# Casting and turning the first rows of a projection kernel between its first products

**Chip, cores, metric.** One core of a Trainium2 chip. The time is device time in microseconds (us). "Span" is the time from the first to the last instruction, about 1.8 us less.

## The reference

```python
batch, seq, hidden = 16, 512, 768
x     = randn(batch, seq, hidden)      # float32, 8192 rows
w_qkv = randn(hidden, 3 * hidden)      # float32
qkv = np.matmul(x, w_qkv)
out = np.stack([q, k, v])              # the three column blocks of qkv, float32
```

## The kernel before

Rows are handled in pairs of 128-row tiles. Pairs 0 to 2 are multiplied directly in bf16; pairs 3 to 31 take a path with seven block products instead of eight. Only the head, the first 20 us of some 361, is touched by the change. In it, each of the six 128-row tiles ("row 1" to "row 6") is loaded, cast to bf16, turned by TensorE (PE) with six transposes into PSUM (the memory that PE writes to), and copied out by VectorE (first three k) and ScalarE (last three). Weights for the first 512 columns come in six k-tiles of 128 x 512. Before the first rows are there, PE runs "dummies", 512-column matmuls on zeros whose results nobody reads. The program order given here is the order on each engine.

```python
def copy_halves(dst, src, two):
    nc.vector.tensor_copy(out=dst[0], in_=src[0])
    if two:
        nc.scalar.activation(dst[1], src[1], ident)
    else:
        nc.vector.tensor_copy(out=dst[1], in_=src[1])

def turn_rows(p, two=True):
    c = xc.pop(p)
    xb[p] = xb_pool.tile([P, KT, 2 * P], bf16, name="xb", tag="xb")
    for r in range(2):
        cols = c[:, r, :].rearrange("m (p j) -> m j p", j=KT)
        ps = ps_pool.tile([P, KT, P], bf16, name="ps")
        for j in range(KT):
            nc.tensor.transpose(ps[:, j, :], cols[:, j, :], eye)
        ks = (slice(0, KH), slice(KH, KT))
        copy_halves([xb[p][:, n, r * P:(r + 1) * P] for n in ks], [ps[:, n, :] for n in ks], two)

# ... loads are issued in the order rows of pair 0, pair 1, k-tiles 0 to 5, remainder weights, pair 2, ...
singles = [((0, ), (0, 1)), ((1, ), (0, 1)), ((0, 1), (2, 3))]      # (k-tiles, row tiles)
singles += [((j, ), range(4)) for j in range(2, KT)]
# ...
busy(11)                 # 11 dummy matmuls on a zero tile
cast_rows(0)
turn_rows(0)
busy(4)
cast_rows(1)
cast_k(0)
cast_k(1)
turn_rows(1)
for j in range(2, KT):
    cast_k(j)
act.activation(w_rem[1][:], st_rem[:, KH:], ident)
dve.tensor_copy(out=w_rem[0][:], in_=st_rem[:, :KH])
# ...
block(0, 0, b1[0], singles, nothing)
rem(0)                   # 12 products with the 256 remaining columns
rem(1)
cast_rows(2, False)
turn_rows(2, False)
block(0, 0, b1[0], halves((4, 5)), nothing)
# ... the next block starts here ("next block" below); pairs 3 to 31 follow after two more
```

## Time and profile before

| | before |
|---|---|
| three timed runs | 362.50, 362.59, 362.67 us |
| the profiled execution | 363.13 us, span 361.3 |
| PE busy | 353.4 us (98%) |
| VectorE / ScalarE / GpSimd busy | 62% / 51% / 48% |

The page's line of the granted TensorE clock shows 9 (90% or more) in all 40 slices. The other lines that carry the argument stand in the prediction.

### The profile page before, as it was taken

How to read it: one execution, taken by the hardware profiler on the slowest of the kernel's cores; microseconds unless marked ns; L12 is line 12 of the kernel's file. 1: busy time of each engine (PE TensorE's matmuls, PEld its weight loads, DVE VectorE, ACT ScalarE, POOL GpSimd, SP SyncE). 2: the span in 40 equal slices, each digit the busy share in tenths (PEclk: the TensorE clock that was granted, in tenths of full speed). 3: DMA queues.
4: the chain of work that ended last, by engine and by line, in shares of the span. 5: the costliest groups of instructions: out<-in, count | busy, mean ns of one | idle time of the engine just before them, and what ended most of it. 6: DMA issues, size and time to landing. Idle time of an engine off the chain costs nothing.

```text
span 361.3 us, 5221 instructions
## 1 busy us (share of the span) xinstructions
PE 353.4 (98%) x1765; PEld 251.0 (69%) x1797; DVE 224.4 (62%) x239; ACT 182.9 (51%) x304; POOL 173.9 (48%) x180
## 2 busy tenths in 40 slices
PE   8999999999999999999999999999999999999995
PEld 3644577777777777777777777777777777777763
DVE  3499826765566765566675565676556676556642
ACT  4547555455454545454545445455545454545452
POOL 0001861746664445664445665444665444666410
PEclk9999999999999999999999999999999999999999
DMA  7999869988898999899899999998989899999666
GB/s 298 405 388 373 286 221 359 331 289 295 278 328 301 294 273 294 276 324 315 280 280 290 281 308 309 291 289 278 292 288 321 295 300 271 297 272 339 264 261 232
DMA packets 80617, 108.08 MB, mean 299 GB/s; under 512 B 4816, under 2 KB 60368, under 8 KB 80592
## 3 DMA queue, kind: packets, MB, share of 16 engines
q1 hardware_dynamic: 65184, 96.35, 80.8%
q10 hardware_dynamic: 15408, 11.41, 9.6%
q8 instruction: 14, 0.23, 0.3%
q14 instruction: 11, 0.09, 0.1%
HBM read 32.24 MB, written 75.50 MB: 298 GB/s over the span
## 4 chain that ended last, share of the span: by engine, by line
PE 96%; ACT 1%; issue 1%; ACTq 0%; DVE 0%
PE ps L212 75%; PE ps L262 11%; PE ps L385 9%; PE ps L365 1%; PE ps L167 1%; ACT o L243 0%; ACTq L303 0%; ACT xb L147 0%; ACT orem L317 0%; DVE xb L145 0%; ACT xc L147 0%; ACTq L319 0%; DVE zero L346 0%; ACTq L317 0%
## 5 line engine op out<-in xcount | busy, mean ns | idle before, releaser
L212 PE MATMUL ps<-t,s 128*128 128x512 f32 x696 | 173.8, 398 | 0.0
L212 PEld LDWEIGHTS ps<-t,s 128*128 128x128 f32 x696 | 130.7, 188 | 29.7
L175 POOL CAST xb<-xf 128x1536 bf16<-128x1536 f32 x29 | 43.8, 1510 | 168.3 <-DVE xf L130 156.0
L240 DVE TENSOR_TENSOR o<-o,ps 128x512 f32<-128x512 f32 x58 | 39.9, 688 | 91.2 <-ACT o L239 91.2
L130 DVE STREAM_TRANSPOSE xf<-xin 128x1536 f32<-128x1536 f32 x29 | 85.5, 2950 | 3.7 <-DMA out_dram<-orem 2.1
L212 PE MATMUL ps<-b,xb 128*128 128x512 bf16 x320 | 82.4, 380 | 1.5
L239 ACT ACTIVATE o<-ps 128x512 f32<-128x512 f32 x58 | 34.8, 600 | 44.2 <-PE ps L212 44.2
L212 PEld LDWEIGHTS <-xb 128*128 128x128 bf16 x348 | 31.7, 98 | 35.6 <-issue 7.3
L233 ACT ACTIVATE o<-ps 128x512 f32<-128x512 f32 x58 | 34.9, 601 | 42.1 <-PE ps L212 39.4
L246 DVE TENSOR_TENSOR o<-o,ps 128x512 f32<-128x512 f32 x58 | 39.9, 688 | 21.3 <-PE ps L212 20.2
L212 PE MATMUL ps<-b,s 128*128 128x512 f32 x174 | 48.7, 389 | 0.0
L262 PE MATMUL ps<-w_rem,xb 128*128 128x256 bf16 x384 | 47.2, 273 | 0.0
L243 ACT ACTIVATE o<-ps 128x512 f32<-128x512 f32 x58 | 34.7, 599 | 24.1 <-PE ps L212 21.3
L226 ACT ACTIVATE o<-ps 128x512 f32<-128x512 f32 x58 | 34.7, 598 | 23.8 <-DVE o L246 20.6
L262 PEld LDWEIGHTS <-xb 128*128 128x128 bf16 x384 | 37.4, 98 | 11.2 <-issue 0.5
L230 DVE TENSOR_TENSOR o<-o,ps 128x512 f32<-128x512 f32 x58 | 36.5, 673 | 5.4 <-PE ps L212 4.1
L212 PEld LDWEIGHTS ps<-b,s 128*128 128x128 f32 x174 | 32.7, 188 | 6.8
L184 POOL TENSOR_TENSOR s<-s,xf 128x384 fp32r<-128x384 f32 x29 | 30.0, 1035 | 2.3
L183 POOL TENSOR_TENSOR s<-xf 128x384 fp32r<-128x384 f32 x29 | 30.9, 1064 | 0.0
L185 POOL TENSOR_TENSOR s<-xf 128x384 fp32r<-128x384 f32 x29 | 29.5, 1017 | 0.0
L187 POOL TENSOR_TENSOR s<-xf,s 128x384 fp32r<-128x384 f32 x29 | 29.5, 1016 | 0.0
L272 ACT ACTIVATE orem<-ps 128x512 f32<-128x512 f32 x31 | 18.5, 598 | 20.7 <-PE ps L262 19.5
(36 smaller groups left out, 129.4 us busy)
## 6 DMA issues: line engine op xcount, KB each, us to landing
out_dram<-o SPq DMA_DIRECT2D x62, 768.0 KB, 4.8
out_dram<-o SPq DMA_DIRECT2D x65, 256.0 KB, 4.1
xin<-in_x_dram SPq DMA_DIRECT2D x62, 192.0 KB, 6.9
xin<-in_x_dram ACTq DMA_DIRECT2D x54, 192.0 KB, 4.4
out_dram<-orem SPq DMA_DIRECT2D x31, 256.0 KB, 5.7
st<-in_w_qkv_dram SPq DMA_DIRECT2D x6, 768.0 KB, 13.1
xin<-in_x_dram SPq DMA_DIRECT2D x3, 768.0 KB, 5.7
st<-in_w_qkv_dram SPq DMA_DIRECT2D x6, 256.0 KB, 6.1
```

Of the source, the lines that this page charges most:

```text
L130: nc.vector.transpose(t[:].rearrange("p j (g b) -> p g j b", b=G), xin.pop(p)[:].rearrange("p g (a j) -> p g j a", a=G),)
L175: nc.gpsimd.tensor_copy(out=xb[p][:], in_=xf[p][:])
L212: nc.tensor.matmul(ps[:], lhs[j], rhs[j], start=(start and j == 0), stop=(j == KH - 1), skip_group_check=True,)
L226: nc.scalar.activation(c11, u.x[:], ident)
L230: nc.vector.tensor_tensor(c11, c11, u.z[:], op=add)
L233: nc.scalar.activation(c12, u.x[:], ident)
L239: nc.scalar.activation(c22, u.x[:], ident)
L240: nc.vector.tensor_tensor(c22, c22, u.y[:], op=add)
L243: nc.scalar.activation(c21, u.x[:], ident)
L246: nc.vector.tensor_tensor(c12, c12, u.y[:], op=add)
L262: nc.tensor.matmul(ps, xb[p][:, j, r * P:(r + 1) * P], w_rem[j // KH][:, j % KH, :], start=(j == 0), stop=(j == KT - 1), skip_group_check= ...
L385: nc.tensor.matmul(ps[n][:], xb[p][:, j, r * P:(r + 1) * P], w[:, j, :], start=(j == 0), stop=(j == KT - 1), skip_group_check=True,)
```

## The change

The intent is to fill PE's waits in the head. Second pair: the transposes of each row stand between the products of k-tile 0 and k-tile 1, which need only the first pair, and VectorE's casts alternate accordingly. Third pair: each row is cast and turned behind one pair's remainder products, and row 5's products run whole before row 6's. The remainder weights' load is split in two. The instructions for PE, VectorE and ScalarE are the same in number.

```diff
-    load_w(st_rem[:], 0, KT, R_OFF, REM)
+    for h in range(2):
+        load_w(st_rem[:, h * KH:(h + 1) * KH], h * KH, KH, R_OFF, REM)
...
-    cast_rows(1)
+    cast_row(1, 0)
     cast_k(0)
+    cast_row(1, 1)
     cast_k(1)
-    turn_rows(1)
-    for j in range(2, KT):
-        cast_k(j)
...
+    def third_row():
+        turn_row(1, 0)
+        cast_k(2)
+
+    def fourth_row():
+        turn_row(1, 1)
+        for j in range(3, KT):
+            cast_k(j)
+        ...                                   # remainder weights' casts
...
-    block(0, 0, b1[0], singles, nothing)
-    rem(0)
-    rem(1)
-    cast_rows(2, False)
-    turn_rows(2, False)
-    block(0, 0, b1[0], halves((4, 5)), nothing)
+    block(
+        0, 0, b1[0],
+        [((0, ), (0, 1)), third_row, ((1, ), (0, 1)), fourth_row, ((0, 1), (2, 3))]
+        + [((j, ), range(4)) for j in range(2, KT)],
+        nothing,
+    )
+    for p in range(2):
+        rem(p)
+        cast_row(2, p, False)
+        turn_row(2, p, False)
+    block(0, 0, b1[0], [(range(KT), (4, )), (range(KT), (5, ))], nothing)
```

More of the change, by code (lines that the diff above doesn't have):

```diff
@@ L151, with cast_row, turn_row @@
     xc = {}
-    def cast_rows(p, two=True):
-        src = xin.pop(p)
-        xc[p] = s_pool.tile([P, 2, K], bf16, name="xc", tag="s")
-        for r in range(2):
-            halves = (slice(0, K // 2), slice(K // 2, K))
-            copy_halves([xc[p][:, r, n] for n in halves], [src[:, r, n] for n in halves], two)
-    def turn_rows(p, two=True):
-        c = xc.pop(p)
-        xb[p] = xb_pool.tile([P, KT, 2 * P], bf16, name="xb", tag="xb")
-        for r in range(2):
-            cols = c[:, r, :].rearrange("m (p j) -> m j p", j=KT)
-            ps = ps_pool.tile([P, KT, P], bf16, name="ps")
-            for j in range(KT):
-                nc.tensor.transpose(ps[:, j, :], cols[:, j, :], eye)
-            ks = (slice(0, KH), slice(KH, KT))
-            copy_halves(
-                [xb[p][:, n, r * P:(r + 1) * P] for n in ks], [ps[:, n, :] for n in ks], two
-            )
+    def cast_row(p, r, two=True):
+        if r == 0:
+            xc[p] = s_pool.tile([P, 2, K], bf16, name="xc", tag="s")
+        halves = (slice(0, K // 2), slice(K // 2, K))
+        copy_halves([xc[p][:, r, n] for n in halves], [xin[p][:, r, n] for n in halves], two)
+    def turn_row(p, r, two=True):
+        if r == 0:
+            xb[p] = xb_pool.tile([P, KT, 2 * P], bf16, name="xb", tag="xb")
+        cols = xc[p][:, r, :].rearrange("m (p j) -> m j p", j=KT)
+        ps = ps_pool.tile([P, KT, P], bf16, name="ps")
+        for j in range(KT):
+            nc.tensor.transpose(ps[:, j, :], cols[:, j, :], eye)
+        ks = (slice(0, KH), slice(KH, KT))
+        copy_halves(
+            [xb[p][:, n, r * P:(r + 1) * P] for n in ks], [ps[:, n, :] for n in ks], two
+        )
     def round_x(p):
@@ L349, with load_k @@
     make_identity(nc, eye)
+    st_0 = tq_pool.tile([P, KT, CB], fp32, name="st0", tag="tq")
+    stage[0, 0, 0], stage[0, 1, 0] = st_0[:, :KH, :], st_0[:, KH:, :]
+    def load_k(j):
+        load_w(st_0[:, j:j + 1], j, 1, Q_OFF[0], CB)
     load_rows(1)
-    load_blocks(0, 0, 1)
+    for j in range(KT):
+        load_k(j)
     st_rem = o_pool.tile([P, KT, REM], fp32, name="str", tag="o")
-    load_w(st_rem[:], 0, KT, R_OFF, REM)
+    for h in range(2):
+        load_w(st_rem[:, h * KH:(h + 1) * KH], h * KH, KH, R_OFF, REM)
     load_rows(2)
-    load_blocks(0, 1)
+    load_blocks(0, 1, KH)
     load_blocks(1, 0)
@@ L378, in block @@
         ps = {}
-        for js, tiles in groups:
+        for group in groups:
+            if callable(group):
+                group()
+                continue
+            js, tiles = group
             for n in tiles:
@@ L399, in halves @@
         return [(range(h * KH, (h + 1) * KH), tiles) for h in range(2)]
-    singles = [((0, ), (0, 1)), ((1, ), (0, 1)), ((0, 1), (2, 3))]
-    singles += [((j, ), range(4)) for j in range(2, KT)]
     act, dve = nc.scalar, nc.vector
-    def cast_k(j):
-        dve.tensor_copy(out=b1[0][:, j, :], in_=stage[0, j // KH, 0][:, j % KH, :])
     def cast_next(q, c, w):
@@ L416 @@
     busy(11)
-    cast_rows(0)
-    turn_rows(0)
+    cast_row(0, 0)
+    cast_row(0, 1)
+    turn_row(0, 0)
+    turn_row(0, 1)
     busy(4)
-    cast_rows(1)
+    cast_row(1, 0)
     cast_k(0)
+    cast_row(1, 1)
     cast_k(1)
-    turn_rows(1)
-    for j in range(2, KT):
-        cast_k(j)
-    act.activation(w_rem[1][:], st_rem[:, KH:], ident)
-    dve.tensor_copy(out=w_rem[0][:], in_=st_rem[:, :KH])
+    def third_row():
[5 more added lines that the diff above has]
+            cast_k(j)
+        dve.tensor_copy(out=w_rem[0][:], in_=st_rem[:, :KH])
+        act.activation(w_rem[1][:], st_rem[:, KH:], ident)
     bt0 = bt_pool.tile([P, KT, CB], bf16, name="bt")
     bt1 = bt_pool.tile([P, KT, CB], bf16, name="bt")
-    block(0, 0, b1[0], singles, nothing)
-    rem(0)
-    rem(1)
-    cast_rows(2, False)
-    turn_rows(2, False)
-    block(0, 0, b1[0], halves((4, 5)), nothing)
+    block(
[3 more added lines that the diff above has]
+        nothing,
+    )
+    for p in range(2):
[3 more added lines that the diff above has]
+    block(0, 0, b1[0], [(range(KT), (4, )), (range(KT), (5, ))], nothing)
     for h in range(2):
```

## The prediction

> **What bounds the kernel now.** I read the page first, then the chain of work that ended last in order of time, then the timeline of the first 22 us (whole, and for the TensorE alone), then busy time by stretch.
>
> The page's busy line and its chain by engine:
>
> ```profile
> PE 353.4 (98%) x1765; PEld 251.0 (69%) x1797; DVE 224.4 (62%) x239; ACT 182.9 (51%) x304; POOL 173.9 (48%) x180
> ...
> PE 96%; ACT 1%; issue 1%; ACTq 0%; DVE 0%
> ```
>
> The TensorE (PE) works for 98% of the span and is 96% of the chain. Only PE time, or an idle hole of PE, can move the end. The change touches only the head, so I looked for holes there. Stretches, in the order us, PE busy, PEld, DVE, ACT, POOL, clock, DMA share, GB/s:
>
> ```profile
> 7.98:8.51 0.53, 0.00 (x2) 0.01 (x1) 0.53 (x3) 0.53 (x3) 0.00 (x0) 1.00 1.08 417
> 8.51:9.30 0.79, 0.79 (x13) 0.77 (x14) 0.44 (x2) 0.36 (x1) 0.00 (x0) 1.00 1.03 397
> 9.30:14.48 5.18, 5.13 (x27) 2.35 (x27) 2.49 (x7) 2.21 (x4) 0.00 (x0) 1.00 1.06 403
> 14.48:17.10 2.62, 2.62 (x26) 2.36 (x25) 1.17 (x4) 2.11 (x5) 0.00 (x0) 1.00 1.05 410
> 17.10:18.05 0.95, 0.83 (x15) 0.69 (x13) 0.42 (x2) 0.60 (x1) 0.00 (x0) 1.00 1.04 403
> 18.05:20.65 2.60, 2.55 (x12) 1.18 (x14) 2.60 (x6) 0.45 (x1) 0.00 (x0) 1.00 1.05 402
> 20.65:44.00 23.35, 23.25 (x108) 10.62 (x109) 21.61 (x12) 15.53 (x23) 9.23 (x6) 1.00 0.99 341
> ```
>
> PE is idle for 0.53 + 0.00 + 0.05 + 0.00 + 0.12 + 0.05 = 0.75 us between 7.98 and 20.65, and then for 0.10 in 23 us. This 0.75 us is all that the change can win; behind it PE is solid. What the holes wait for, from the same chain by time and from PE's timeline:
>
> ```profile
> 8.04 0.42 ACT xc L147
> ...
> 17.63 0.37 DVE xb L145
> ...
> 8.51 0.95 PE L167 MATMUL ps<-eye,xc 128*128 128x128 bf16 x12 [0.53 <-ACT xc L147]
> 9.30 5.34 PE L385 MATMUL ps<-b,xb 128*128 128x512 bf16 x23
> ```
>
> The fence's first two lines are pieces of the chain (start, us, what). The first is ScalarE's cast of the second half of the third row, for which the 12 transposes of the second pair wait after the last dummy matmul. The second is the copy of the fifth row's transposes out of PSUM, for which the first product of the third pair waits. The last two show the transposes standing ahead of all products of the first block.
>
> One subtlety: an end of a matmul is modelled, and the next can start before it. The four dummy matmuls start at 6.95 (timeline); at 5.18/24 = 0.216 us per 512-column matmul (from which I take 0.05 as one small issue hole, so 0.2137 each) PE could take the next at 6.95 + 4 x 0.2137 = 7.81. Measured by starts, the hole before 8.51 is therefore 0.70, not 0.53.
>
> **What the Trainium skill says.** "TensorE: Matmul & The Clock Gate", section "Wait — 56ns, not 53.3ns?", gives 215.7 ns start to start for 512 columns on a warm array; this trace has 213.7. The same page, "Part 1: The HAM clock gate", says the clock falls back only after an idle window of about 3.4 us; the largest hole here is 0.7 us and the granted clock is 1.00 in every stretch above, so I expect no gain or loss by clock. "VectorE: DVE Perf Modes", "The TRN2 errata", would make a cast of 384 fp32 elements at two per cycle (58 + 192)/0.96 = 260 ns; the trace has 353 from start to end, but 270 from one start to the next (14.85, 15.12, 15.39). I use the trace's: 0.27 per step for 384 elements, 0.34 per step and 0.42 of length for a 512-element k-tile. "DMA: Bandwidth & Descriptors", "Queues, rings and completion order", says that descriptors of a ring are taken in ring order. The change keeps the order of all bytes loaded and only splits the remainder weights' load in two. Queues are at 1.03 to 1.08 of their share from 8 us on, so arrivals stay where they are; the trace agrees in so far as the loads are used in the order of their issue.
>
> **The change part by part.** Counts on PE, ScalarE and VectorE do not change (the built program has the same number of matmuls, transposes, casts and copies); SyncE gets one more load. All is order.
>
> Part 1, second pair. VectorE's order becomes cast of row 3 (half), k-tile 0, cast of row 4, k-tile 1, instead of both casts first. Row 3's cast starts at 7.43 as before; k-tile 0 at 7.43 + 0.27 = 7.70, done at 8.12, one semaphore step of 0.05 (as 18.00 to 18.05 in the chain) makes 8.17. k-tile 1: 7.70 + 0.34 + 0.27 = 8.31, done 8.73. PE now:
> - two products of k-tile 0 (they need only rows 1 and 2, ready) 8.17 to 8.60;
> - six transposes of row 3: ScalarE's cast half is ready at 8.46, so no wait; 0.79/12 = 0.066 each, to 9.00;
> - two products of k-tile 1 to 9.43; six transposes of row 4 (its cast ends 8.35 + 0.52 = 8.87) to 9.82;
> - row 3's two first k-products to 10.25. Its copy out of PSUM begins 0.57 after the first transpose (8.51 to 9.08 before), at 9.17, so it is ready;
> - row 4's: the copy begins 9.43 + 0.57 = 10.00 and ends 10.36, with the semaphore 10.42 (17.63 to 18.05 before is 0.42 too). PE waits 0.17, a new hole;
> - the other 18 products, 18 x 0.2137 = 3.85, and the issue hole of 0.05: 14.32.
> k-tiles 2 to 5 are cast at about 9.44, 10.27, 10.61 and 10.95 and needed at 10.85, 11.70, 12.55 and 13.41; no wait. The remainder weights are cast by ScalarE at 12.91 to 13.75, before 14.32. So the first remainder product starts at 14.32 instead of 14.48: minus 0.16. The hole of 0.70 has become 0.36 (7.81 to 8.17) plus 0.17.
>
> Part 2, third pair. The remainder of pair 1 takes 12 x 0.109 = 1.31, to 15.63. Row 5 was loaded and is cast on VectorE at 14.85 to 15.47 (the load sets 14.85, as before), so its six transposes run 15.63 to 16.03 without a wait. The second remainder runs 16.03 to 17.34. Meanwhile VectorE copies row 5 (16.16 and 16.43) and casts row 6 (16.70 and 16.97, done 17.32, visible at 17.37). Row 6's transposes 17.37 to 17.77: a hole of 0.03. Then all six k of row 5 (1.28) to 19.05, in which row 6's copies (17.90 to 18.53) hide entirely, and row 6 to 20.33. Before, the next block began at 20.65. Part 2 thus removes the holes of 0.12 and 0.05 and leaves 0.03: about minus 0.16.
>
> Sum: 20.65 - 20.33 = 0.32 us. The next block's weights (VectorE casts at about 18.45 instead of 18.70) are ready. Behind it PE has nothing to wait for, so the shift should carry through 29 rounds to the end, where the stores' drain moves with it. 362.59 - 0.32 = 362.27, said as 362.3.
>
> **Rivals.**
> - *The gain is the whole 0.75 or a little more.* For it: the intent of the change, and that PE's start could be filled if k-tile 0 were cast by 7.8. Against: VectorE is strictly in order and its copy of row 2 only starts at about 7.15; row 4's copy is awaited at once. It would give 361.8 to 361.9.
> - *A new wait takes the place of the old ones.* Row 4's copy and row 6's cast both stand on VectorE behind something that itself waits for PE; if a transpose-to-copy turn takes 0.2 more than I took, twice, the gain is gone: 362.6 to 362.8. For it: row 6's margin is minus 0.03. Against: VectorE has 1 to 2 us free before 12.9 and its steps are well known from before.
> - *The gain is lost later*, because loads, stores or VectorE's chain of sums set the pace. For it: DMA share is 0.99 in 20.65 to 44 and VectorE is busy 21.6 of 23.35 us there. Against: PE has 0.10 us of idle there, and the chain of waits behind holds only PE until 353 us. It would give 362.6.
> - *Split load or more alternation of transposes and products costs.* Four more switches on PE; if each cost 0.05, 0.2: 362.5. At 8.51 to 9.30 and 17.10 the switches of before cost nothing I can see.
>
> **Range and chances.** The holes bound the gain from above at about 0.8 (361.8); failures of two of my VectorE turns bound it below at about plus 0.2 (362.8). The three runs of before spread by 0.17 and agreement between chips is not known from them, so I leave 361.7 to 362.9 for 8 in 10. A change of 2% is 7.25 us, ten times the holes; nothing in the profile makes so much. Faster 0.005, within 0.99, slower 0.005.
>
> **What would show it.** In the changed profile: the first product at about 8.17, ahead of the second pair's first transpose at about 8.60; a hole of about 0.17 before row 4's first product near 10.4, with VectorE's copy of it as the releaser; first remainder near 14.3; six transposes at 15.6 and six at 17.4; the next block near 20.33; and the first round's remainder of the steady loop about 0.3 earlier, with the round's 10.74 us unchanged. I would be wrong if the first product waits for the load of k-tile 0 or 1 (their margins against the casts are small), if a bank of PSUM is not yet emptied by ScalarE when a transpose wants it, or if the shift at 20.65 does not reach the end.

## The result, and the profile after

After: 362.64 us median (362.61 to 362.78, six runs). Before, on the same chip: 362.58 (362.50 to 363.30, six runs). The ratio is 1.0, interval 0.9987 to 1.0012: no difference.

The predicted 0.32 us is not in the time. Yet the profile shows it. PE's timeline of the kernel after (start, us, engine, line, operation, count, and the idle time before with its releaser):

```profile
1.19 3.94 PE L371 MATMUL ps<-zero 128*128 128x512 bf16 x11 [1.19 <-DVE zero L344]
5.57 0.95 PE L165 MATMUL ps<-eye,xc 128*128 128x128 bf16 x12 [0.44 <-ACT xc L147]
6.36 1.03 PE L371 MATMUL ps<-zero 128*128 128x512 bf16 x4
8.00 0.59 PE L396 MATMUL ps<-b,xb 128*128 128x512 bf16 x2 [0.61 <-DVE b L417]
...
9.53 4.67 PE L396 MATMUL ps<-b,xb 128*128 128x512 bf16 x20
14.04 1.47 PE L260 MATMUL ps<-w_rem,xb 128*128 128x256 bf16 x12
15.47 0.54 PE L165 MATMUL ps<-eye,xc 128*128 128x128 bf16 x6
15.84 1.47 PE L260 MATMUL ps<-w_rem,xb 128*128 128x256 bf16 x12
17.26 0.54 PE L165 MATMUL ps<-eye,xc 128*128 128x128 bf16 x6
17.63 2.75 PE L396 MATMUL ps<-b,xb 128*128 128x512 bf16 x12
20.22 4.05 PE L396 MATMUL ps<-bt,xb 128*128 128x512 bf16 x18
```

The next block starts at 20.22 instead of 20.65, and the span is 360.9 instead of 361.3: the 0.4 arrives at the end undiminished. So the question is not where a gain was lost later, but whether the profile of before was a fair baseline. Its first two lines say why not:

```profile
1.19 4.88 PE L365 MATMUL ps<-zero 128*128 128x512 bf16 x11 [1.19 <-DVE zero L346]
5.86 1.26 PE L167 MATMUL ps<-eye,xc 128*128 128x128 bf16 x12
```

The same 11 dummies take 4.88 us there and 3.94 in the profile after. One by one, the dummies of before step by 0.43 us to the last; in the profile after, seven are slow (the seventh in part) and the last four step by 0.216. I call this passage from 0.43 to 0.216 us a step the opening of the clock, and matmuls before it slow. In before the transposes start 0.3 later, and nine of them are still slow, the ninth in part (0.107 us a step, then 0.056): 1.26 for twelve against 0.95. Nothing of this shows in the clock column, which reads 1.00 in both traces for 1.19 to 5.00 us. And the chain of the kernel after, in order of time, shows what holds its head instead:

```profile
1.74 5.76 DMA st<-in_w_qkv_dram
7.49 0.02 issue
7.52 0.44 DVE b L417
7.96 0.04 issue
8.00 0.59 PE ps L396 x2
```

That is the load of k-tile 0 and its cast. VectorE sat idle for 0.28 us before this cast, waiting for the load, so PE's start can be somewhat later without moving it.

### The profile page after: what moved, and what is told of

The parts are those of the page before. It is cut to its first block, busy times and chain, and to the rows that moved or that the text cites. A ratio compares the mean times of both kernels' runs of the same rounds, so it can differ in the third digit from the quotient of the medians.

```text
span 360.9 us, 5252 instructions
## 1 busy us (share of the span) xinstructions
PE 354.3 (98%) x1797; PEld 250.2 (69%) x1797; DVE 224.7 (62%) x239; ACT 182.5 (51%) x304; POOL 173.5 (48%) x180
## 4 chain that ended last, share of the span: by engine, by line
PE 96%; DMA 2%; ACT 1%; ACTq 0%; SPq 0%; issue 0%; DVE 0%
PE ps L210 75%; PE ps L260 11%; PE ps L396 9%; DMA st<-in_w_qkv_dram 2%; PE ps L165 0%; ACT o L241 0%; ACTq L301 0%; SPq L141 0%; ACT orem L315 0%; DVE b L417 0%; ACTq L317 0%; ACTq L315 0%
## 5 line engine op out<-in xcount | busy, mean ns | idle before, releaser
L210 PE MATMUL ps<-b,xb 128*128 128x512 bf16 x348 | 84.9, 380 | 0.0
L244 DVE TENSOR_TENSOR o<-o,ps 128x512 f32<-128x512 f32 x58 | 39.9, 688 | 21.4 <-PE ps L210 20.2
```

Of the source, the lines that this page charges most:

```text
L210: nc.tensor.matmul(ps[:], lhs[j], rhs[j], start=(start and j == 0), stop=(j == KH - 1), skip_group_check=True,)
L244: nc.vector.tensor_tensor(c12, c12, u.y[:], op=add)
```

## The experiments

**Theory A**: the profile of before caught an execution whose TensorE clock opened late; the usual execution is shorter, and in it the change gains nothing. **Theory B**: the span did shrink, and time outside it grew. Later runs ask what each half of the change does. I and II are two chips. Times are lowest, median and highest.

| run | chip | runs | lowest | median | highest |
|---|---|---|---|---|---|
| before | I | 11 | 362.49 | 362.82 | 363.31 |
| before_again | I | 5 | 362.56 | 362.75 | 363.09 |
| before_15 | I | 5 | 362.75 | 362.83 | 363.72 |
| after_15 | I | 5 | 362.67 | 362.82 | 363.20 |
| before_8 | I | 6 | 362.50 | 363.62 | 363.71 |
| before | II | 10 | 362.45 | 362.62 | 363.35 |
| after_again | II | 5 | 362.62 | 362.65 | 362.84 |
| part1 | II | 5 | 362.54 | 362.58 | 362.69 |
| part2 | II | 5 | 362.64 | 362.65 | 362.86 |
| fill | II | 5 | 362.13 | 362.19 | 362.26 |
| fill_second | II | 5 | 362.62 | 362.64 | 362.75 |
| fill_third | II | 6 | 362.31 | 362.34 | 362.60 |
| fill_15 | II | 4 | 362.46 | 362.92 | 363.16 |
| kfirst | II | 4 | 362.74 | 362.77 | 363.28 |

(The first four runs on chip II were compared with nine runs of before, median 362.67; one was added for the last four.) All were correct.

**before_again** is the kernel before, unchanged, so there is no diff.

> The kernel before, unchanged, for its spans and a second profile. Theory A (the profile of before on record is of a late execution: its clock opened only after all 11 dummy matmuls, so the first transposes started at 5.86 instead of about 5.5): most executions have spans of 360.7 to 360.9 at 362.5 to 362.6 us, a few are 0.4 to 0.7 longer; in a profile of a usual execution some dummies are 0.21 apart, the first transposes start by 5.6, the second pair's near 7.95, the first product near 8.75 and the next block near 20.1. Theory B (the change did shorten the span by 0.4 and time outside the span grew by as much): every span is 361.2 to 361.4 at 362.6, and the profile repeats 8.51 and 20.65.

The spans of all 16 executions of this kernel on chip I run from 360.7 to 361.5, and time minus span is about 1.8 us throughout; nothing outside the span changed. B is out. The new profile fell in an execution of 362.56 us (span 360.8). I call such an execution usual, which is only half true: of the 32 recorded times of before, 15 are at most 362.6, 8 are 363.0 or more, and the rest lie between. Theory A's "most executions" at 360.7 to 360.9 was too much: on chip I it was 7 of 16. PE's timeline:

```profile
1.19 4.40 PE L365 MATMUL ps<-zero 128*128 128x512 bf16 x11 [1.19 <-DVE zero L346]
5.58 0.95 PE L167 MATMUL ps<-eye,xc 128*128 128x128 bf16 x12
6.37 1.03 PE L365 MATMUL ps<-zero 128*128 128x512 bf16 x4
7.92 0.95 PE L167 MATMUL ps<-eye,xc 128*128 128x128 bf16 x12 [0.52 <-ACT xc L147]
8.70 5.34 PE L385 MATMUL ps<-b,xb 128*128 128x512 bf16 x24
13.88 2.78 PE L262 MATMUL ps<-w_rem,xb 128*128 128x256 bf16 x24
16.50 0.83 PE L167 MATMUL ps<-eye,xc 128*128 128x128 bf16 x12
17.45 2.76 PE L385 MATMUL ps<-b,xb 128*128 128x512 bf16 x12
20.05 2.32 PE L385 MATMUL ps<-bt,xb 128*128 128x512 bf16 x10
```

From the second pair on, everything stands 0.6 us earlier than in the profile on record, of which 0.28 is the later start of the first transposes and the rest their slowness, passed on through VectorE's copy (6.15 against 6.74), ScalarE's copies (6.54 against 7.13) and ScalarE's cast. Against this execution the kernel after is 0.17 late at the next block.

**before_15 and after_15** delay PE on purpose.

```diff
-    busy(11)
+    busy(15)
```

> The kernel before with 15 dummy matmuls ahead of the first transposes instead of 11, so that PE reaches them about 0.4 us late (11 dummies end near 5.0 in a usual execution, four more at 0.21 make 5.9) whatever the clock. Theory A: this makes every execution like the late one: first transposes near 5.9, next block at 20.4 to 20.7, 362.9 to 363.2 us, that is plus 0.3 to 0.6 against before. Theory B: 8.51 and 20.65 are the usual ones and already hold such a start, so the time goes up by at most 0.1 if the dummies were ended by the clock only, or by the full 0.85 of four dummies beyond 5.86, to 363.4.

> The kernel after with the same 15 dummies. Theory A: the first product waits for k-tile 0's cast at 8.00, and PE is free from about 7.2, so 0.3 to 0.4 us of lateness is absorbed: the first product stays at 8.0 to 8.05, the next block at 20.2 to 20.3, the time within 0.1 of 362.64. The change is then worth 0.3 to 0.5 in late executions and nothing in usual ones. Theory B gives no reason for after_15 to be cheaper than before_15: both shift alike.

after_15's profile has its clock open during the seventh dummy and starts the first transposes at 5.75; the first product stays at 8.00 and the next block at 20.23, as put down. Its lowest time is 0.05 above that of after_again on the other chip. before_15's lowest is 0.26 above before's on the same chip. So where the clock opens early, four more dummies cost the kernel before about 0.26 and the kernel after about 0.05; these are lowest times of few runs, the second across two chips. The medians do not separate (362.83 and 362.82), my "every execution" was wrong, and after_15 stayed within 0.1 of 362.64 in two of five: in a late execution both kernels lose more than the slack. before_15's profile is one, with twelve of its 15 dummies slow (the twelfth in part, the clock opening near 6.1 us) and a next block at 21.24:

```profile
1.19 5.81 PE L365 MATMUL ps<-zero 128*128 128x512 bf16 x15 [1.19 <-DVE zero L346]
6.84 0.83 PE L167 MATMUL ps<-eye,xc 128*128 128x128 bf16 x12
```

**before_8** starts with fewer dummies (`busy(8)` for `busy(11)`).

> The kernel before with 8 dummies instead of 11: even all cold they end at 1.19 + 8 x 0.427 = 4.6, before the first cast lands at 5.45, so a late clock cannot hold the first transposes back; it can only make them slow (0.107 each instead of 0.066). Theory A: median 362.4 to 362.6, and the long executions of 363.1 to 363.3 go or shrink to within 0.3 of the median. Theory B: no change of median, 362.6, and the same long ones as the control.

A miss. Five of six executions took 363.5 to 363.7. The profile shows PE waiting 0.77 us for the first cast and everything after it slow, up to about 9.8 us:

```profile
5.55 1.48 PE L167 MATMUL ps<-eye,xc 128*128 128x128 bf16 x12 [0.77 <-ACT xc L147]
6.83 1.91 PE L365 MATMUL ps<-zero 128*128 128x512 bf16 x4
8.54 1.48 PE L167 MATMUL ps<-eye,xc 128*128 128x128 bf16 x12
```

Four dummies take 1.91 instead of 1.03, transposes 0.107 each instead of 0.066 on average. Fewer dummies do not merely leave PE idle, they go with a later opening. Whether the idle gap is the reason, or that three matmuls fewer came before the transposes, this run can't tell, as both changed together. The run shows what it was not meant for: a later opening can cost this kernel about 1 us (363.70 here, 362.50 in the one short execution, which has no profile).

**after_again** is the kernel after, unchanged.

> The kernel after, unchanged, beside the kernel before on one chip, for the spread over executions. Theory A (the clock's opening decides how long the kernel before takes, and the kernel after has slack for it): spans of before 360.7 to 361.5, spans of after within 360.8 to 361.1 in nearly all executions, so the highest falls by 0.3 or more while the lowest rises by 0.1 (next block at 20.22 against 20.05 in usual executions). Rival C (the change only moves the spread by chance): both spread alike, 0.6 to 0.8 us.

Spans 360.8 to 361.1 against 360.7 to 361.6 for before; time spread 0.22 against 0.90 us. Its profile fell on an execution with ten slow dummies, and yet the first product starts at 8.01. So the change trades about 0.15 us in the best executions for 0.5 in the worst, and the medians meet (362.65 and 362.67). With five executions of one and nine of the other the spread's size is rough; that the highest fell is also what the first comparison shows (362.78 against 363.30). Taken together, none of 11 executions of after exceeds 362.84, and 11 of 32 of before do.

**part1** keeps the second pair's interleaving alone.

```diff
-    for p in range(2):
-        rem(p)
-        cast_row(2, p, False)
-        turn_row(2, p, False)
-    block(0, 0, b1[0], [(range(KT), (4, )), (range(KT), (5, ))], nothing)
+    rem(0)
+    rem(1)
+    for r in range(2):
+        cast_row(2, r, False)
+    for r in range(2):
+        turn_row(2, r, False)
+    block(0, 0, b1[0], halves((4, 5)), nothing)
```

> Only the first half of the change: second pair interleaved with the first k-tiles, third pair as before. In a usual execution: first product 8.00, first remainder 14.04 (as after; before 13.88), both remainders to 16.66, twelve transposes, the wait for the copy (stretch of 0.95 as before), products at 17.61, next block at 20.2. So against the kernel before it is 0.15 slower in a usual execution and the two parts of the loss sit in the second pair: the wait for k-tile 0's cast (8.00, where before PE already turned the second pair from 7.92) and the wait of 0.17 for the fourth row's copy. Rival D (the second half of the change is what costs): part1 alone would be faster than before, next block at 19.9 or less.

**part2** keeps the third pair's alone.

```diff
     cast_row(1, 0)
-    cast_k(0)
     cast_row(1, 1)
+    cast_k(0)
     cast_k(1)
-    def third_row(): ...
-    def fourth_row(): ...
+    turn_row(1, 0)
+    turn_row(1, 1)
+    for j in range(2, KT):
+        cast_k(j)
...
-        [((0, ), (0, 1)), third_row, ((1, ), (0, 1)), fourth_row, ((0, 1), (2, 3))]
+        [((0, ), (0, 1)), ((1, ), (0, 1)), ((0, 1), (2, 3))]
```

> Only the second half: third pair's rows turned among the direct columns, second pair as before. First remainder at 13.88 as in the kernel before; but the fifth row's casts end at 15.41 as its load lands near 14.7, so its transposes start at 15.47 and not at 15.2, and from there all is as in the kernel after: next block at 20.2. So this half also costs 0.15 in a usual execution, since the landing of the third pair's rows and two casts on VectorE set 15.47 whatever comes earlier. Rival D': the second half gains its 0.16 as I predicted, next block at 19.9.

Lines of part1, then of part2:

```profile
8.05 0.59 PE L396 MATMUL ps<-b,xb 128*128 128x512 bf16 x2 [0.58 <-DVE b L417]
14.10 2.78 PE L260 MATMUL ps<-w_rem,xb 128*128 128x256 bf16 x24
20.27 2.11 PE L396 MATMUL ps<-bt,xb 128*128 128x512 bf16 x9
```

```profile
8.70 5.34 PE L396 MATMUL ps<-b,xb 128*128 128x512 bf16 x24
13.88 1.47 PE L260 MATMUL ps<-w_rem,xb 128*128 128x256 bf16 x12
15.45 0.54 PE L165 MATMUL ps<-eye,xc 128*128 128x128 bf16 x6
20.21 2.10 PE L396 MATMUL ps<-bt,xb 128*128 128x512 bf16 x9
```

Each half alone ends where the whole ends, at 20.2 to 20.3, against 20.05 in a usual execution of before: D and D' fall. In the first half PE gives up turning the second pair at 7.92 for products that wait until 8.00, and later waits for row 4's copy. In the second half, row 5's transposes no longer stand behind both remainders (16.50 before) but behind one, which ends before its casts do; 15.45 is set by the landing and by two casts on VectorE. Both lose about 0.16, and the two losses do not add.

**fill** fills the change's own waits.

```diff
-        [((0, ), (0, 1)), third_row, ((1, ), (0, 1)), fourth_row, ((0, 1), (2, 3))]
-        + [((j, ), range(4)) for j in range(2, KT)],
+        [((0, ), (0, 1)), third_row, ((1, ), (0, 1)), fourth_row,
+         ((0, 1), (2, )), ((2, ), (0, 1)), ((0, 1), (3, )), ((2, ), (2, 3))]
+        + [((j, ), range(4)) for j in range(3, KT)],
...
-    for p in range(2):
-        rem(p)
-        cast_row(2, p, False)
-        turn_row(2, p, False)
+    rem(0)
+    cast_row(2, 0, False)
+    cast_row(2, 1, False)
+    ps = ps_pool.tile([P, 2, REM], fp32, name="ps")
+    for r in range(2):
+        rem_row(1, r, ps[:, r, :])
+        turn_row(2, r, False)
+    ...                                       # copy out and store, as in rem
```

> The kernel after with its three new waits filled: the first two tiles' products of k-tile 2 stand between the third and the fourth row's first products (closing the 0.18 at 9.96), and the second remainder is cut by rows: remainder of pair 1, first row of the second remainder, turn row 5, second row, turn row 6, with both rows cast at once (closing 0.12 and 0.11 at 15.35 and 17.15). Theory A: first remainder at 13.86, row 5's transposes at 15.8, row 6's at 16.85, next block at 19.8, span 360.4 to 360.6, 362.2 to 362.4 us, that is 0.25 under the best executions of before. Rival E (the waits are set by arrivals that only move along): next block stays at 20.1 to 20.2.

```profile
1.19 4.88 PE L371 MATMUL ps<-zero 128*128 128x512 bf16 x11 [1.19 <-DVE zero L344]
8.10 0.59 PE L396 MATMUL ps<-b,xb 128*128 128x512 bf16 x2 [0.40 <-DVE b L417]
13.94 2.13 PE L260 MATMUL ps<-w_rem,xb 128*128 128x256 bf16 x18
15.91 0.50 PE L165 MATMUL ps<-eye,xc 128*128 128x128 bf16 x6
16.90 0.50 PE L165 MATMUL ps<-eye,xc 128*128 128x128 bf16 x6
19.82 2.54 PE L396 MATMUL ps<-bt,xb 128*128 128x512 bf16 x11
```

The times put down were met within 0.11, in an execution with all eleven dummies slow. The median is 362.19: 0.46 under after_again, and even its highest (362.26) is under the lowest of before (362.45). The reported ratio to before is 0.9984 (0.9972 to 0.9997). It is far from 2%, but it is the one version here whose interval lies clear of 1 on the fast side. Rival E falls.

**fill_second and fill_third** take one filling each: the first part of fill's diff, and the second.

> The kernel after with only the first filling: products of k-tile 2 for the first two tiles ahead of the fourth row's first products. Theory A with the third pair's arrival as a floor: first remainder at 13.86 to 13.9 (0.18 earlier than after), but row 5's transposes stay at 15.45 to 15.5 as its load and casts end at 15.41, so the next block stays at 20.2 and the time at 362.6 to 362.7: a hole filled ahead of an arrival is worth nothing. Rival F (PE alone sets the pace): next block 20.05, 0.18 less time.

> The kernel after with only the second filling: the second remainder cut by rows. Theory A: first remainder 14.04 as after, row 5's transposes at 16.0 (after 18 remainder products, 14.04 + 1.97), row 6's at 17.0, next block at 20.0, 362.4 (0.23 less than after). Rival F: the same; with fill_second it tells whether the two gains add (F) or whether the first needs the second (A): fill 0.41, fill_second 0, fill_third 0.23.

```profile
14.02 1.47 PE L260 MATMUL ps<-w_rem,xb 128*128 128x256 bf16 x12
15.45 0.54 PE L165 MATMUL ps<-eye,xc 128*128 128x128 bf16 x6
20.20 2.11 PE L396 MATMUL ps<-bt,xb 128*128 128x512 bf16 x9
```

These are fill_second's lines. Filling the first wait alone changes nothing: 362.64 against 362.65, with row 5's transposes at 15.45. Filling the third pair's waits alone gives 0.31 in the medians, both give 0.46: the first needs the second, as theory A has it. (fill_second's remainder stands at 14.02, not 13.86 to 13.9, as its first product was late, at 8.18, after slow transposes; so the trace shows the floor but not the full earlier arrival at it.) fill_third's profiled execution was a longer one (362.54, first product at 8.20), so its lines, 20.12 at the next block, are not to be compared to a tenth. The clock does not explain its length: it had opened by the first transposes, at 5.53. k-tile 0 landed late, and VectorE waited for it:

```profile
7.72 0.43 DVE L417 CAST b<-st 128x512 bf16<-128x512 f32 x1 [0.27 <-DMA st<-in_w_qkv_dram]
```

That is 0.2 later than in the profile after (7.52). So landings, too, differ between executions, and how much of the spread in executions without a profile is the clock's is not known.

**fill_15** is fill with `busy(15)`.

> The filled version with 15 dummies instead of 11, to see how much lateness it takes: as in after_15, an execution whose clock opens early ends its dummies at 5.75 and loses nothing (362.1 to 362.25), one whose clock opens late ends them at up to 1.19 + 15 x 0.427 = 7.6 and loses up to 0.5 to 0.8 (as the 363.1 and 363.2 of after_15). Were the lateness of no account the spread would stay within 0.15.

362.46 at the lowest and 363.16 at the highest: fill, too, pays when the first product is late (8.10 in fill's profile, at 362.26). Its profiled execution (362.85) has twelve slow dummies, the twelfth in part, and the first product at 8.70. With four runs none was at 362.25 or below, so the part on early openings was not met.

**kfirst** moves k-tile 0 ahead of the second pair, in fill.

```diff
+    load_k(0)
     load_rows(1)
-    for j in range(KT):
+    for j in range(1, KT):
         load_k(j)
...
     cast_row(0, 1)
+    cast_k(0)
     turn_row(0, 0)
...
-        [((0, ), (0, 1)), third_row, ((1, ), (0, 1)), fourth_row,
+        [((0, ), (0, 1)), third_row, fourth_row, ((1, ), (0, 1)),
```

> The filled version with k-tile 0 loaded and cast ahead of the second pair's rows (its landing and cast at 7.5 to 8.0 set the first product). k-tile 0 then lands near 5.6 and pair 1 near 7.5. First products at 7.2 (behind the four dummies), then a wait for the second pair's casts, transposes of both rows from 8.15 to 8.9, products of k-tile 1 from 8.9, first remainder at 13.7, next block at 19.65: 0.15 less than fill, 362.05. Rival G (arrival of both is what counts, the order only moves the wait): equal to fill, 362.2.

Slower than fill by 0.6 (362.77). k-tile 0 is cast at 5.62 as meant, but the second pair came later than in either theory:

```profile
8.22 0.63 DVE L145 CAST xc<-xin 128x384 bf16<-128x384 f32 x2 [0.51 <-DMA xin<-in_x_dram]
```

It is cast at 8.22 instead of 7.5, and the third pair at 15.50 instead of 14.89 in fill. Between 4 and 8 us the DMA engines moved 357 to 411 GB/s, against 402 to 412 in fill; I estimate that as 0.26 us of transfers, less than half of the delay. Why swapping a 256 KB and a 768 KB load costs the rest is open. The clock opened late in this profile (7.1 us), but VectorE sat idle for 0.51 us before 8.22 until the second pair landed, so the clock does not explain that delay. Rival G is not told apart by it.

## Why the prediction was right in its class and wrong in its gain

**The baseline: the step that failed.** The prediction took PE's holes from a trace whose execution lasted 363.13, and subtracted them from 362.59, the median of others. Its sum "20.65 - 20.33 = 0.32" was near the mark against that execution: the profiles differ by 0.43 at the next block and by 0.4 in the span. But 20.65 is that of a late execution; before_again measures 20.05. Against that the kernel after is later by 0.28 by its own forecast (20.33), or by 0.17 by the measured 20.22, that is no gain; the lowest times of the two kernels on chip II differ by 0.17 (362.62 and 362.45). That the class was right is no luck, since all holes together were a tenth of 2%; but the range, 361.7 to 362.9, holds the forecast gain and no gain alike.

**"I expect no gain or loss by clock."** Wrong, and it is why the baseline passed unexamined. I argued from the largest hole and from the granted clock of 1.00, a column that reads 1.00 also where matmuls of 512 columns stand 0.43 us apart. The Trainium skill, "TensorE: Matmul & The Clock Gate", "Part 1: The HAM clock gate", states what I left aside: the window is free-running, so the number of cold matmuls varies from run to run. Here 7 (after and after_15), 9 (before_again), 10 (after_again), 12 (before_15), and in before on record all 11 and nine transposes were slow.

**The matmul's step.** The prediction took 213.7 ns from the trace, by setting 0.05 us aside as an issue hole. There is no such hole: the products start 0.216 us apart throughout, and fill's 20 products without a wait take 9.63 to 13.94, 0.2155 each, so the 215.7 that it quotes is what the trace has. Of its 0.75 us of holes, 0.10 were none. In its sum this is worth about 0.03: the third pair's twelve products were counted as 2.56 us and take 2.59.

**Part 1.** Predicted 8.17, 14.32; measured 8.00, 14.04. k-tile 0 was cast at 7.52, not 7.70, since the copies ahead of it did not run late; below that its own landing is the floor (cast at once behind it in the chain above). The new wait for row 4's copy is there as predicted (0.17): VectorE's copy starts at 9.73 and ends at 10.09, and 18 products follow at 10.14.

**Part 2.** Predicted 15.63, 17.37 and 20.33; measured 15.47, 17.26 and 20.22. The prediction had row 5's casts in time by 0.16; with part 1 ending earlier, the casts became the floor (15.41) and PE waits 0.12 there and 0.11 before row 6, where 0.03 was allowed. part2 shows that PE's earlier arrival is worth nothing there: its first remainder ended near 15.19 (13.88 + 1.31), and row 5 was still turned at 15.45.

**Rivals.** "A new wait takes the place of the old ones" was the nearest, and gave the right time, 362.6 to 362.8; but the waits that mattered were the landing of k-tile 0 and of the third pair, not longer turns on VectorE. That the first product might wait for k-tile 0's load stood among the prediction's signs of being wrong. "The gain is lost later" is refuted: what is at 20.2 arrives at the end in every pair of profiles (20.05 with 360.8, 20.22 with 360.9, 19.82 with 360.5). "Alternation costs" is refuted too: six transposes between products step by 0.33 to 0.37 us, under the 0.40 allowed.

## What to carry to other kernels

Before reading holes of tenths of a microsecond out of a profile, compare the profiled execution's own time with the median, and take a second profile if they differ by as much as the holes. Work interleaved to fill a wait gains only down to the next arrival, so fill the waits behind the last arrival first, and give a row that has not landed enough other work ahead of it, in pieces as small as the wait. A schedule can also be worth having for its spread: the same median came with a quarter of the range.

## What the Trainium skill lacked or had wrong

- "TensorE: Matmul & The Clock Gate", Part 1: it puts the opening near 4 us of activity, give or take 0.5, though it also gives 6, 11 or 14 cold matmuls for one kernel. With PE fed from 1.19 us on, it came during the seventh dummy, about 2.7 us later (after_15), and only after eleven dummies and twelve transposes, 5.9 us later (kfirst), far more than half a microsecond either way.
- The same page calls the ramp below 1% of a span and not worth fitting. True in size (0.25%, 362.45 to 363.35 us), but it exceeds many a change to a tuned kernel: the whole spread of before (0.90 us, not all of it shown to be the clock's) was larger than every difference of medians on either chip.
- The same page warns that a trace's clock events can be unreliable, but no page says that the granted clock of a profile page can read 1.00 while the array is still cold (1.00 from 1.19 to 5.00 us in before and after, with matmuls 0.43 us apart).
- The same page asks for about 3.4 us of sustained activity before the opening; it gives no number for the gap that spoils it. In before_8 a gap of 0.77 us in the warm-up went with an opening near 9.8 us (cause not shown).
- "VectorE: DVE Perf Modes", "The TRN2 errata": its row for VectorE gives 260 ns for a cast of 384 fp32 elements; the trace has 353 from start to end and 270 from start to start. This is not wrong in the page as a whole: it says itself that the row is too low for a single operation and that the fixed term is about 150 cycles, which makes an estimate of 356 ns.
